# A decoder layer on one core: u also stored by columns, weights stored in the pieces read, three halves of the expert sums kept in PSUM

## The chip, the core and the metric

The kernel runs on one core of a Trainium2 chip. The metric is the device time of one execution in microseconds (us): three runs of the kernel before took 3350.16, 3357.07 and 3360.35 us, median 3357.07. The core has five engines that work side by side, each on its own list of instructions in a fixed order: TensorE (PE, matrix products), VectorE (DVE), ScalarE (ACT), GpSimd (POOL) and SyncE (SP, which here only issues transfers). Sixteen DMA engines move data between DRAM and the core's two memories, SBUF (128 partitions) and PSUM (eight banks of 128 x 512 float32, where PE writes its sums).

## The reference

One layer for 1024 tokens of 1024 values, in float32:

```python
h += W_out [ RMSNorm(attention) ; RMSNorm(convolution) ]      # both from RMSNorm(h) @ w_in
h += PEER(RMSNorm(h))
h += sigmoid(RMSNorm(h) @ w_ple_gate) * (p @ w_ple_proj)
out = RMSNorm(h)
```

PEER is a retrieval among 16384 single-neuron experts. Per token, each of 8 heads scores 2 x 128 keys (`xn @ peer_wq`, then a product with the keys), takes the 16 best of each half and then the 16 best of their sums; these 128 experts per token have gates g by a softmax. The result is

```python
h_e   = xn . u[e]                      # u: 16384 x 1024
y     = sum over the token's experts of gelu(h_e) * g_e * v[e]
```

The arrays are handed to the kernel by the host; what the host does to their layout before the launch is not part of the time.

## The kernel before

The 1024 tokens are 8 tiles of 128. Five groups of tiles (0; 1, 2; 3, 4; 5, 6; 7) go through the **front** one after the other: input projection (`qkv`, `convolve`), attention, convolution, output projection (`project`), key search (`search`) and the choice of experts (`combine`). Each product with a weight reads the weight afresh for the group, in pieces of 512 KB, three buffers (`w_piece`, L246). `token_major` (L254) reads 256 rows by 512 columns as [128, 2, 512], so runs of 512 columns, 2 KB, in DRAM; `channel_major` (L267) reads 1024 rows by 128 columns as [128, 8, 128], so runs of 512 B.

PEER is done in two ways. For tiles 0, 1, 2 and 7 (`FEW`) the experts are **gathered** (`gather_u` L602, `gather_v` L619): one indirect DMA from POOL's queue (L595) brings for each of the 128 tokens one row of u or v, 4 KB each, 512 KB in all, into one of six buffers, and DVE multiplies and sums it (L608 for u, L624 for v). That is 128 gathers of u and then 128 of v per tile, 1024 in all. Each use is put at least five gathers behind its own (`LAG`).

For tiles 3 to 6 (`ALL`) **all experts run** (`dense`, L695): 512 tokens against 128 chunks of 128 experts. Beforehand each tile's gates are laid into a matrix in DRAM (`gate_matrix`, L636). For float32 accuracy at a faster product, both sides of each product are split into a high and a low part, and three products are summed. A chunk needs

- `columns` (L702): the chunk's rows of u are loaded (512 KB), transposed by PE in eight blocks of 128 x 128 into two PSUM banks (`put`, L710), and each half is split by ACT (`uh`, L712) and DVE (`ul`, L714) into three buffers of half a chunk for each part. It is called one chunk ahead of its use;
- 24 products into a PSUM bank `ph` (L738 to L740), a gelu by ACT (L742), the gates by DVE (L746), a split of the result (`ah` L748, `al` L750);
- the chunk's rows of v, loaded into one of two buffers and split (`vh` L756, `vl` L758).

After every four chunks (a group of the dense sums, 32 in all) the sums over these 512 experts are made for 4 tiles x 2 halves of 512 columns, 12 products each (L769 to L771). Seven of these eight halves go through two PSUM banks `py` and are added to h by DVE each time (L773); one, tile 3's first half, stays in its own bank `kept_y` through all 32 groups and is added once (L774).

At the last group, `read` (L894) frees the inputs' memory and loads the last weights (`wt`). The **tail** is `embed` (L776) for each tile: a transposed and normed h (`pt_ple`, L792, evicted as `x3T`), 16 products per half with the gate's weight (`plg`, L802) and 4 with p (`plp`, L808) as the profile counts them, sigmoid, product, norm, output. For the dense tiles its PSUM tiles come from four banks that the inputs of the last sums leave; for the gathered tiles everything goes through the one bank `acc`. The gathered tiles 0 to 2 are embedded in the middle of the dense sums, with weights loaded for them (`we`).

The order on each engine and in each DMA queue is not written out by hand: a planner (the tile framework) makes it before the launch from the order of the program, priorities, buffers and estimated costs. The gathers are written last in the program, so they are fitted in where the rest leaves room; the engines then follow that order and wait where data or a buffer is not there.

Of the kernel before, what the change touches and what calls it, by code (L numbers as in the profile page):

```python
# [20 lines left out]
P = 128  # L21
# [4 lines left out]
GROUPS = ((0,), (1, 2), (3, 4), (5, 6), (7,))  # tiles of 128 tokens that go through the mixers together  # L26
# [4 lines left out]
FEW = (0, 1, 2, 7)  # tiles whose experts are gathered  # L31
ALL = (3, 4, 5, 6)  # tiles for which all experts run
# [19 lines left out]
GROUP = 4  # chunks of 128 experts whose outputs are summed in PSUM  # L52
BT = 32  # tokens of a block of the gate matrix
# [3 lines left out]
# Of the sums of two sorted lists of 16, the 16 largest lie where (i + 1) * (j + 1) <= 16.  # L57
# [14 lines left out]
def _constants():  # L72
    c = np.zeros((P, C_END), np.float32)
    # Columns of key blocks, the farthest first: distance of query q from key column s.
    dist = np.arange(P)[:, None] + (SEQ - P) - np.arange(SEQ)[None, :]
    mult = np.zeros(dist.shape)
    for window, step in PATTERNS:
        mult += (dist >= 0) & (dist <= window) & (dist % step == 0)
    c[:, C_BIAS : C_BIAS + SEQ] = np.where(mult > 0, math.sqrt(DH) * np.log(np.maximum(mult, 1)), NEG)
    c[:, C_ID : C_ID + P] = np.eye(P)  # L80
    c[:, C_IOTA : C_IOTA + P] = np.arange(P)
    freq = np.float32(THETA) ** (-np.arange(0, 2 * ROT, 2, dtype=np.float32) / np.float32(2 * ROT))
    c[:, C_FREQ : C_FREQ + ROT] = freq
# [19 lines left out]
def tile_layer(ctx, tc, t, consts, out):  # L103
# [7 lines left out]
    by_k = lambda name: t[name][0].rearrange("(k p) c -> p k c", p=P)  # L111
    w_in, w_out, w_q, w_g, w_p = (by_k(n) for n in ("w_in", "w_out", "peer_wq", "w_ple_gate", "w_ple_proj"))
# [28 lines left out]
    def rstd(srcs, n, name, junk=None, pool=small):  # L141
        """1 / sqrt(mean(src^2) + eps) along the free axis, a column for each src."""
# [13 lines left out]
    def transpose_to(dst, src, n, name, ps_tile, gain=None):  # L156
        """dst [P, n, P] = the n blocks of src [P, n * P], transposed; times gain [P, n]."""
# [35 lines left out]
    def load_tables():  # L193
        # Rows to columns: the gains of the mixers' norms, the convolution's taps and bias.
# [8 lines left out]
        # Rotary angles, brought into [-pi, pi] by exact multiples of parts of 2 pi.  # L203
# [42 lines left out]
    def w_piece(src, name):  # L246
        """A piece of a weight: [P, k, columns] in 4 KB of each partition."""
        _, k, c = src.shape
        w = mpool.tile([P, 1024], F32, tag="w", name=name, bufs=3)
        w = w.rearrange("p (k c) -> p k c", k=k)  # L250
# [53 lines left out]
    def qkv(g, xT):  # L304
# [16 lines left out]
        token_major(xT, w_in, DA, f"k{g}", done_k)  # L321
        token_major(xT, w_in, 0, f"q{g}", done_q)
        token_major(xT, w_in, 2 * DA, f"v{g}", lambda j, a: S.copy(vt[:, GROUPS[g][j], :], a))
        return qT

    def convolve(g, xT):
        """The gated units, channels on partitions, and the convolution's taps over them."""
        gn = xT.shape[2]
        glus = []
        for c in range(NCT):  # L330
            pg = channel_major(xT, w_in, 3 * DA + DC + c * P, f"gt{g}_{c}")
            sg = mpool.tile([P, GN], F32, tag="t2", name=f"sg{g}_{c}", bufs=3)[:, :gn]
            S.activation(sg, pg, AF.Sigmoid)
            pa = channel_major(xT, w_in, 3 * DA + c * P, f"a{g}_{c}")
# [28 lines left out]
    def attend(g, qT):  # L363
        """One softmax over the keys, each counted as often as the patterns hold it."""
# [42 lines left out]
    def mixed(g, ys, cT):  # L407
        """Both halves of the mixers' output, normed and transposed."""
# [31 lines left out]
    def project(g, yT):  # L440
        """h1 = x + y @ w_out."""
# [8 lines left out]
        for f in range(2):  # L450
            token_major(
                yT, w_out, f * 512, f"o{g}_{f}", lambda j, a: V.tensor_tensor(h1[j][:, half(f)], a, h1[j][:, half(f)], ALU.add)
# [15 lines left out]
    def search(g, x2T):  # L468
        """The 16 best keys of each head's halves."""
# [6 lines left out]
        for hp in range(PH // 2):  # L476
            qT = []
            for r in range(4):
                n = 4 * hp + r
                pq = channel_major(x2T, w_q, n * P, f"pq{g}_{n}")  # L480
# [19 lines left out]
    def combine(nm, vals, idxs, opool, gbufs):  # L500
        """For one tile: i1, i2 (bf16) and gates (f32), [P, head, rank]."""
# [24 lines left out]
        # Gates: softmax over the 16.  # L526
# [7 lines left out]
        # From a candidate's place to its row i and column j, then to the keys there.  # L534
# [8 lines left out]
        def total(dst, a, dt=BF16):  # L543
            """The sums over the last axis; its partial sums of more than two terms are of type dt."""
# [13 lines left out]
        # Row i: the number of starts up to the place; sums over the steps from one row to the next.  # L558
# [60 lines left out]
    def gather_v(i, ex, act, y):  # L619
        """The sum over experts of their rows of v, a rank of all tokens at a time."""  # L620
# [15 lines left out]
    def gate_matrix(gp, j, i1, i2, gate):  # L636
        """G[i1, i2, token] of one tile in DRAM, in blocks of BT tokens: each token's gates at its experts."""
# [42 lines left out]
    def wide_input(h1, xh, xl):  # L680
        """The normed input of the tiles for which all experts run, transposed, as a sum of two float32r."""
# [13 lines left out]
    def dense(du, dp, dus, dps, h1, xh, xl, read):  # L695
        """h1 += PEER(xn), over all experts, GROUP chunks of 128 at a time."""
        phs, puts, pys = bank(dus, "ph", 2), bank(dus, "put", 2), bank(dps, "py", 2)
        # One tile's sums stay in PSUM through all chunks; its halves come where the others' banks are emptied.
        kept_y = dps.tile([P, 512], F32, name="kept_y")
        order = [(1, 0), (1, 1), (0, 1), (2, 0), (0, 0), (2, 1), (3, 0), (3, 1)]  # L700

        def columns(c):  # L702
            """The chunk's rows of u, transposed, as a sum of two float32r: halves of the k blocks."""
            u = du.tile([P, D], F32, tag="u", name=f"u{c}", bufs=2)
            nc.sync.dma_start(u, u_d[rows(c), :])
            uh, ul = [], []
            for b in range(0, KD, 4):
                pt = puts(f"put{c}_{b}")
                for i in range(4):
                    nc.tensor.transpose(pt[:, rows(i)], u[:, rows(b + i)], ident)  # L710
                hi = du.tile([P, 512], F32R, tag="uh", name=f"uh{c}_{b}", bufs=3)
                S.copy(hi, pt)  # L712
                lo = du.tile([P, 512], F32R, tag="ul", name=f"ul{c}_{b}", bufs=3)
                V.tensor_tensor(lo, pt, hi.bitcast(F32), ALU.subtract)  # L714
                uh.append(hi)
                ul.append(lo)
            return uh, ul

        ready = columns(0)
        for c0 in range(0, NK, GROUP):  # L720
# [10 lines left out]
            for c in range(c0, c0 + GROUP):  # L731
# [4 lines left out]
                for k in range(KD):  # L736
                    hi, lo = uh[k // 4][:, rows(k % 4)], ul[k // 4][:, rows(k % 4)]
# [25 lines left out]
            for j, f in order:  # L763
                py = kept_y if (j, f) == (0, 0) else pys(f"py{c0}_{j}_{f}")
                for e in range(GROUP):
                    first, last_e = e == 0, e == GROUP - 1
                    if (j, f) == (0, 0):
# [4 lines left out]
                if (j, f) != (0, 0):  # L772
                    V.tensor_tensor(h1[j][:, half(f)], py, h1[j][:, half(f)], ALU.add)  # L773
        V.tensor_tensor(h1[0][:, half(0)], kept_y, h1[0][:, half(0)], ALU.add)  # L774

    def embed(pool, bufs, i, h, g_fin, ps_tile, weight):  # L776
        """out = finalnorm(h + sigmoid(rmsnorm(h) @ w_g) * (p @ w_p)) for one tile; weight(k, f): rows 2k of both, a half."""
# [6 lines left out]
        # Transposed and divided by the root mean square by a product with a diagonal matrix.  # L784
# [11 lines left out]
        for f in range(2):  # L796
            pg = ps_tile(f"plg{i}_{f}")
# [7 lines left out]
            pp = ps_tile(f"plp{i}_{f}")  # L805
# [10 lines left out]
    def embed_weight(pool, name, kq, f, bufs=1):  # L816
        w = pool.tile([P, 2, 512], F32, tag=name.rstrip("0123456789") if bufs > 1 else name, name=f"{name}_{kq}_{f}", bufs=bufs)
        nc.sync.dma_start(w, w_p[:, :, half(f)] if kq == KD // 2 else w_g[:, 2 * kq : 2 * kq + 2, half(f)])
        return w

# [73 lines left out]
    def read():  # L894
        """What follows takes the place of the inputs of the last sums, beside which it starts."""
# [8 lines left out]
        tails.extend((tail, bank(tail_ps, "pg", 4)))  # L904
# [4 lines left out]
    tiles = [embed(tails[0], ND, ALL[j], h1[j], g_fin, tails[1], lambda k, f: kept[k, f]) for j in range(ND)]  # L909
    # As they are done: the front of a tile's work beside the sums of the next, then the products.  # L910
    for j in (1, 0, 2, 1, 0, 3, 2, 3):
        next(tiles[j])
    for i, y in gather_all():
        with tc.high_priority():
# [4 lines left out]
            for _ in embed(ep, 1, i, y, g_fin, acc, weight):  # L919
                pass  # L920
# [3 lines left out]
    "x", "p", "positions", "norm_mix", "w_in", "conv_w", "conv_b", "conv_ln_g", "conv_ln_b", "g_attn_out", "g_conv_out",  # L924
    "w_out", "norm_ffn", "peer_wq", "sub_keys", "expert_u", "expert_v", "norm_ple", "w_ple_gate", "w_ple_proj", "final_norm",
]

# [19 lines left out]
```

## Time and profile before

| | |
|---|---|
| median of three runs | 3357.07 us (3350.16 to 3360.35) |
| span of the profiled execution, first to last instruction | 3356.7 us (the page gives no other time of it) |
| PE busy | 2938.0 us, 88% |
| DVE busy | 2675.1 us, 80% |
| POOL busy | 1615.9 us, 48% |
| ACT busy | 1222.0 us, 36% |
| moved by DMA | 901.62 MB, 268 GB/s over the span |

A row of the costliest groups gives line, engine, operation, `out<-in`, shapes and count, then the busy time in us and the mean in ns, then the idle time of the engine right before these instructions and what ended most of it. PE's durations there overlap, since matmuls are pipelined; starts in the timeline tell the pace. A row of waits reads: who waited <- for whom: us in total, times, longest. A row of stretches gives start and end, length, then busy us (and instructions) of the engines that the text names, TensorE's granted clock (1 is full), the mean busy share of the DMA engines and GB/s. A row of the chain of waits gives start, length and the work that the end hung on at that time. The 40 slices are of 84 us, each digit the busy share in tenths.

### The profile page before, as it was taken

The numbers are of one execution on the slowest core, as the hardware profiler recorded it, in microseconds if no ns is written. First come the engines' busy times: TensorE is split into PE (matmuls) and PEld (weight loads), VectorE is DVE, ScalarE is ACT, GpSimd is POOL, SyncE is SP. The second block draws the span as 40 slices with busy tenths as digits, with TensorE's granted clock in tenths as the row PEclk, the third lists the DMA queues.
The fourth block names the chain that finished last, engine by engine and source line by source line (L and its number), as shares of the span: only waits on it lengthen the run. The fifth ranks groups of instructions, "written<-read, shape, count | busy, mean of one in ns | idle before, by whom it ended". The sixth has DMA issues, their size and how long they took to land.

```text
span 3356.7 us, 39363 instructions
## 1 busy us (share of the span) xinstructions
PE 2938.0 (88%) x12867; PEld 2253.1 (67%) x12867; DVE 2675.1 (80%) x5416; ACT 1222.0 (36%) x2316; POOL 1615.9 (48%) x1392
## 2 busy tenths in 40 slices
PE   6687888799789399978999999798999989999998
PEld 3454366367457299966777777577877757777763
DVE  3269779989979766677899888688988978888882
ACT  4436335434534477742223223222222233222234
POOL 1237645443543543325565655454655645555650
PEclk9898989899899699979999999999999999999999
DMA  6575894594486364369999989998989999999880
GB/s 199 169 263 186 315 320 126 186 324 138 138 301 219 119 213 163 144 232 346 342 345 347 343 312 327 325 323 325 347 317 337 325 327 340 342 322 326 309 332 32
DMA packets 425439, 901.62 MB, mean 269 GB/s; under 512 B 27866, under 2 KB 217714, under 8 KB 423186
## 3 DMA queue, kind: packets, MB, share of 16 engines
q0 software_dynamic: 147456, 536.94, 44.2%
q1 hardware_dynamic: 274512, 358.81, 32.0%
q10 hardware_dynamic: 3266, 3.36, 0.3%
q8 instruction: 102, 1.67, 0.2%
q14 instruction: 103, 0.84, 0.1%
HBM read 857.06 MB, written 41.94 MB: 268 GB/s over the span
## 4 chain that ended last, share of the span: by engine, by line
PE 36%; DMA 20%; DVE 18%; issue 14%; POOL 9%; ACT 3%; POOLq 0%; ACTq 0%; SPq 0%; DVEq 0%
PE pG L676 7%; DMA v<-in_expert_v_dram 5%; PE pq L272 4%; DMA w_pq<-in_peer_wq_dram 3%; POOL v L595 3%; DVE cc L358 3%; POOL u L595 3%; DVE u L608 3%; DMA v<-in_expert_v_dram,ex 3%; PE plg L802 2%; DVE gy L624 2%; DMA u<-in_expert_u_dram,ex 2%; PE o L263 2%; PE py L769 2%; PE py L771 2%
## 5 line engine op out<-in xcount | busy, mean ns | idle before, releaser
L595 POOL DMA_INDIRECT u<-in_expert_u_dram,ex x512 | 640.5, 1251 | 710.3 <-DVE hk L608 458.5
L595 POOL DMA_INDIRECT v<-in_expert_v_dram,ex x512 | 661.5, 1292 | 593.5 <-DVE gy L624 433.5
L624 DVE SCALAR_TENSOR_TENSOR gy<-v,ga,gy 128x1024 f32<-128x1024 f32 x512 | 662.7, 1294 | 36.6 <-DMA v<-in_expert_v_dram,ex 29.0
L608 DVE CUSTOM_DVE_ANT_0 u<-u,gxn 128x1024 f32<-128x1024 f32 x512 | 619.1, 1229 | 35.2 <-DMA u<-in_expert_u_dram,ex 34.7
L738 PE MATMUL ph<-xh,uh 128*128 128x512 f32 x1024 | 427.3, 417 | 0.0
L739 PE MATMUL ph<-xl,uh 128*128 128x512 f32 x1024 | 415.2, 405 | 0.0
L740 PE MATMUL ph<-xh,ul 128*128 128x512 f32 x1024 | 414.4, 405 | 0.1
L756 ACT CAST vh<-v 128x1024 fp32r<-128x1024 f32 x128 | 131.5, 1052 | 701.5 <-PE py L771 522.1
L769 PE MATMUL py<-vh,ah 128*128 128x512 f32 x896 | 353.8, 396 | 9.8 <-ACT ah L748 8.3
L770 PE MATMUL py<-vl,ah 128*128 128x512 f32 x896 | 349.6, 393 | 0.0
L771 PE MATMUL py<-vh,al 128*128 128x512 f32 x896 | 348.1, 392 | 0.0
L352 POOL TENSOR_TENSOR side<-side,tap 128x256 f32<-128x256 f32 (+1 forms) x300 | 217.1, 725 | 184.5 <-ACT tap L351 166.3
L272 PE MATMUL pq<-x2T,w_pq 128*128 128x256 f32 (+1 forms) x1280 | 254.7, 350 | 35.4 <-DMA w_pq<-in_peer_wq_dram 35.3
L272 PEld LDWEIGHTS pq<-x2T,w_pq 128*128 128x128 f32 x1280 | 220.6, 200 | 60.7 <-DMA w_pq<-in_peer_wq_dram 16.6
L740 PEld LDWEIGHTS ph<-xh,ul 128*128 128x128 f32 x1024 | 200.4, 196 | 47.2 <-issue 2.7
L738 PEld LDWEIGHTS ph<-xh,uh 128*128 128x128 f32 x1024 | 202.4, 198 | 41.1 <-issue 2.2
L739 PEld LDWEIGHTS ph<-xl,uh 128*128 128x128 f32 x1024 | 201.2, 196 | 41.4 <-issue 2.7
L710 PE MATMUL put<-cst,u 128*128 128x128 f32 x1024 | 149.0, 285 | 89.4 <-DVE ul L714 77.0
L758 DVE TENSOR_TENSOR vl<-v,vh 128x1024 fp32r<-128x1024 f32 x128 | 156.0, 1219 | 75.0 <-ACT vh L756 74.4
L712 ACT CAST uh<-put 128x512 fp32r<-128x512 f32 x256 | 149.6, 584 | 167.9 <-PE ph L739 137.2
L769 PEld LDWEIGHTS py<-vh,ah 128*128 128x128 f32 x896 | 169.1, 189 | 55.5 <-ACT ah L748 16.1
L710 PEld LDWEIGHTS put<-cst,u 128*128 128x128 f32 x1024 | 124.3, 146 | 117.2 <-DVE ul L714 88.9
(264 smaller groups left out, 5223.1 us busy)
## 6 DMA issues: line engine op xcount, KB each, us to landing
u<-in_expert_u_dram SPq DMA_DIRECT2D x128, 512.0 KB
v<-in_expert_v_dram SPq DMA_DIRECT2D x128, 512.0 KB
w_pq<-in_peer_wq_dram SPq DMA_DIRECT2D x80, 512.0 KB
gate_d<-stage SPq DMA_DIRECT2D x16, 2048.0 KB
gt<-gate_d SPq DMA_DIRECT2D x64, 512.0 KB
w_o<-in_w_out_dram SPq DMA_DIRECT2D x40, 512.0 KB
we<-in_w_ple_gate_dram SPq DMA_DIRECT2D x24, 512.0 KB
w_k<-in_w_in_dram SPq DMA_DIRECT2D x20, 512.0 KB
```

The costliest lines, as they stand in the source:

```text
L272: nc.tensor.matmul(a, w[:, k, :], xT[:, k, :], start=k == 0, stop=k == KD - 1)
L595: d = G.indirect_dma_start(out=e, out_offset=None, in_=table, in_offset=bass.IndirectOffsetOnAxis(ap=index, axis=0))
L608: uses(V.tensor_tensor_reduce(out=e, in0=e, in1=xn, scale=1.0, scalar=0.0, op0=ALU.mult, op1=ALU.add, accum_out=hk[:, k : k + 1]))
L624: uses(V.scalar_tensor_tensor(y, e, act[:, k : k + 1], y, ALU.mult, ALU.add))
L676: nc.tensor.matmul(pg[:, rows(e)], o2[:, :, e], parts[e], start=True, stop=True)
L710: nc.tensor.transpose(pt[:, rows(i)], u[:, rows(b + i)], ident)
L738: nc.tensor.matmul(ph, hi, xh[:, k, :], start=k == 0, stop=False)
L739: nc.tensor.matmul(ph, hi, xl[:, k, :], start=False, stop=False)
L740: nc.tensor.matmul(ph, lo, xh[:, k, :], start=False, stop=k == KD - 1)
L769: nc.tensor.matmul(py, ah[e][:, rows(j)], vh[e][:, half(f)], start=first, stop=False)
L770: nc.tensor.matmul(py, ah[e][:, rows(j)], vl[e][:, half(f)], start=False, stop=False)
L771: nc.tensor.matmul(py, al[e][:, rows(j)], vh[e][:, half(f)], start=False, stop=last_e)
```

## The change

1. **u by columns.** Beside the rows of u (which the gathers still read) the host lays u out a second time, chunk by chunk, transposed: 128 partitions x 1024 values, one run of 4 KB for each partition. `columns` loads such a chunk and has no transposes; ACT and DVE split it as one piece of 128 x 1024 from SBUF, into two buffers of a whole chunk for each part. The two PSUM banks `put` are gone.
2. **Weights in pieces.** The host lays out every weight in the pieces that the kernel reads, each piece 128 partitions x 4 KB in one run. The pieces hold the same values, and as many are loaded as before.
3. **Three kept halves.** Tile 3's both halves and tile 6's first half stay in PSUM through all groups; five halves are added in each group and three once at the end. The order of the eight halves alternates kept and other ones in its middle.
4. **Banks of the tail.** The dense tiles' transposes get two banks instead of four; their products (and tile 7's) get four banks `late`, which come free when the banks of the dense sums are closed.

Comments are taken out as well, which changes no instruction. The diff, cut to its core:

```diff
+    uT_d = t["uT"]
-    by_k = lambda name: t[name][0].rearrange("(k p) c -> p k c", p=P)
-    w_in, w_out, w_q, w_g, w_p = (by_k(n) for n in ("w_in", "w_out", "peer_wq", "w_ple_gate", "w_ple_proj"))
+    w_qkv, w_ag, w_out, w_q, w_g, w_p = (t[n] for n in ("w_qkv", "w_ag", "w_out", "peer_wq", "w_ple_gate", "w_ple_proj"))
...
     def token_major(xT, w_k, c0, name, done):
-            w = w_piece(w_k[:, 2 * kq : 2 * kq + 2, c0 : c0 + 512], f"w_{name}_{kq}")
+            w = w_piece(w_k[c0, kq], f"w_{name}_{kq}").rearrange("p (i c) -> p i c", i=2)
...
     def channel_major(xT, w_k, c0, name):
-        w = w_piece(w_k[:, :, c0 : c0 + P], f"w_{name}")
+        w = w_piece(w_k[c0], f"w_{name}").rearrange("p (k c) -> p k c", k=KD)
...
     def dense(du, dp, dus, dps, h1, xh, xl, read):
-        phs, puts, pys = bank(dus, "ph", 2), bank(dus, "put", 2), bank(dps, "py", 2)
-        kept_y = dps.tile([P, 512], F32, name="kept_y")
-        order = [(1, 0), (1, 1), (0, 1), (2, 0), (0, 0), (2, 1), (3, 0), (3, 1)]
+        phs, pys = bank(dus, "ph", 2), bank(dps, "py", 2)
+        kept_y = {jf: dps.tile([P, 512], F32, name=f"kept_y{jf[0]}{jf[1]}") for jf in ((0, 0), (0, 1), (3, 0))}
+        order = [(1, 0), (1, 1), (0, 0), (2, 0), (0, 1), (2, 1), (3, 0), (3, 1)]
         def columns(c):
             u = du.tile([P, D], F32, tag="u", name=f"u{c}", bufs=2)
-            nc.sync.dma_start(u, u_d[rows(c), :])
-            uh, ul = [], []
-            for b in range(0, KD, 4):
-                pt = puts(f"put{c}_{b}")
-                for i in range(4):
-                    nc.tensor.transpose(pt[:, rows(i)], u[:, rows(b + i)], ident)
-                hi = du.tile([P, 512], F32R, tag="uh", name=f"uh{c}_{b}", bufs=3)
-                S.copy(hi, pt)
-                lo = du.tile([P, 512], F32R, tag="ul", name=f"ul{c}_{b}", bufs=3)
-                V.tensor_tensor(lo, pt, hi.bitcast(F32), ALU.subtract)
-                uh.append(hi)
-                ul.append(lo)
-            return uh, ul
+            nc.sync.dma_start(u, uT_d[c])
+            hi = du.tile([P, D], F32R, tag="uh", name=f"uh{c}", bufs=2)
+            S.copy(hi, u)
+            lo = du.tile([P, D], F32R, tag="ul", name=f"ul{c}", bufs=2)
+            V.tensor_tensor(lo, u, hi.bitcast(F32), ALU.subtract)
+            return hi, lo
...
-                if (j, f) != (0, 0):
+                if (j, f) not in kept_y:
                     V.tensor_tensor(h1[j][:, half(f)], py, h1[j][:, half(f)], ALU.add)
-        V.tensor_tensor(h1[0][:, half(0)], kept_y, h1[0][:, half(0)], ALU.add)
+        for (j, f), py in kept_y.items():
+            V.tensor_tensor(h1[j][:, half(f)], py, h1[j][:, half(f)], ALU.add)
-    def embed(pool, bufs, i, h, g_fin, ps_tile, weight):
+    def embed(pool, bufs, i, h, g_fin, ps_tile, ps_out, weight):
-            pg = ps_tile(f"plg{i}_{f}")
+            pg = ps_out(f"plg{i}_{f}")
-            pp = ps_tile(f"plp{i}_{f}")
+            pp = ps_out(f"plp{i}_{f}")
...
-        tails.extend((tail, bank(tail_ps, "pg", 4)))
+        tails.extend((tail, bank(tail_ps, "pg", 2)))
     dense(du, dp, dus, dps, h1, xh, xl, read)
     den_ps.close()
     den.close()
-    tiles = [embed(tails[0], ND, ALL[j], h1[j], g_fin, tails[1], lambda k, f: kept[k, f]) for j in range(ND)]
+    late_ps = ctx.enter_context(tc.tile_pool(name="late_ps", bufs=1, space=PSUM))
+    late = bank(late_ps, "late", 4)
+    tiles = [embed(tails[0], ND, ALL[j], h1[j], g_fin, tails[1], late, lambda k, f: kept[k, f]) for j in range(ND)]
...
-            for _ in embed(ep, 1, i, y, g_fin, acc, weight):
+            for _ in embed(ep, 1, i, y, g_fin, acc, late if i == FEW[-1] else acc, weight):
...
+def _by_token(w):
+    k, c = w.shape
+    return w.reshape(k // 256, 2, P, c // 512, 512).transpose(3, 0, 2, 1, 4).reshape(c // 512, k // 256, P, 1024)
+def _by_channel(w):
+    k, c = w.shape
+    return w.reshape(k // P, P, c // P, P).transpose(2, 1, 0, 3).reshape(c // P, P, k)
...
+    give("w_qkv", _by_token(w_in[:, : 3 * DA]))
+    give("w_ag", _by_channel(w_in[:, 3 * DA :]))
+    for name in ("w_out", "w_ple_gate", "w_ple_proj"):
+        give(name, _by_token(np.asarray(inputs[name])[0]))
+    give("peer_wq", _by_channel(np.asarray(inputs["peer_wq"])[0]))
+    give("uT", _by_channel(np.asarray(inputs["expert_u"])[0].T))
```

More of the change, by code (lines that the diff above doesn't have):

```diff
@@ L246, in w_piece @@
     def w_piece(src, name):
-        _, k, c = src.shape
         w = mpool.tile([P, 1024], F32, tag="w", name=name, bufs=3)
-        w = w.rearrange("p (k c) -> p k c", k=k)
         nc.sync.dma_start(w, src)
@@ L319, in done_q @@
             transpose_to(qT[:, j], q, H // 2, f"q{i}", tps)
-        token_major(xT, w_in, DA, f"k{g}", done_k)
-        token_major(xT, w_in, 0, f"q{g}", done_q)
-        token_major(xT, w_in, 2 * DA, f"v{g}", lambda j, a: S.copy(vt[:, GROUPS[g][j], :], a))
+        token_major(xT, w_qkv, 1, f"k{g}", done_k)
+        token_major(xT, w_qkv, 0, f"q{g}", done_q)
+        token_major(xT, w_qkv, 2, f"v{g}", lambda j, a: S.copy(vt[:, GROUPS[g][j], :], a))
         return qT
@@ L330, in convolve @@
         for c in range(NCT):
-            pg = channel_major(xT, w_in, 3 * DA + DC + c * P, f"gt{g}_{c}")
+            pg = channel_major(xT, w_ag, NCT + c, f"gt{g}_{c}")
             sg = mpool.tile([P, GN], F32, tag="t2", name=f"sg{g}_{c}", bufs=3)[:, :gn]
             S.activation(sg, pg, AF.Sigmoid)
-            pa = channel_major(xT, w_in, 3 * DA + c * P, f"a{g}_{c}")
+            pa = channel_major(xT, w_ag, c, f"a{g}_{c}")
             glu = apool.tile([P, TAPS - 1 + GN], F32, tag="glu", name=f"glu{g}_{c}", bufs=NCT - 1)[:, : TAPS - 1 + gn]
@@ L451, in project @@
             token_major(
-                yT, w_out, f * 512, f"o{g}_{f}", lambda j, a: V.tensor_tensor(h1[j][:, half(f)], a, h1[j][:, half(f)], ALU.add)
+                yT, w_out, f, f"o{g}_{f}", lambda j, a: V.tensor_tensor(h1[j][:, half(f)], a, h1[j][:, half(f)], ALU.add)
             )
@@ L479, in search @@
                 n = 4 * hp + r
-                pq = channel_major(x2T, w_q, n * P, f"pq{g}_{n}")
+                pq = channel_major(x2T, w_q, n, f"pq{g}_{n}")
                 q = mpool.tile([P, GN], F32, tag="pqT", name=f"pqT{g}_{n}", bufs=4)[:, :gn]
@@ L736, in dense @@
                 for k in range(KD):
-                    hi, lo = uh[k // 4][:, rows(k % 4)], ul[k // 4][:, rows(k % 4)]
+                    hi, lo = uh[:, rows(k)], ul[:, rows(k)]
                     nc.tensor.matmul(ph, hi, xh[:, k, :], start=k == 0, stop=False)
@@ L763, in dense @@
             for j, f in order:
-                py = kept_y if (j, f) == (0, 0) else pys(f"py{c0}_{j}_{f}")
+                py = kept_y[j, f] if (j, f) in kept_y else pys(f"py{c0}_{j}_{f}")
                 for e in range(GROUP):
                     first, last_e = e == 0, e == GROUP - 1
-                    if (j, f) == (0, 0):
+                    if (j, f) in kept_y:
                         first, last_e = first and c0 == 0, last_e and c0 + GROUP == NK
@@ L817, in embed_weight @@
         w = pool.tile([P, 2, 512], F32, tag=name.rstrip("0123456789") if bufs > 1 else name, name=f"{name}_{kq}_{f}", bufs=bufs)
-        nc.sync.dma_start(w, w_p[:, :, half(f)] if kq == KD // 2 else w_g[:, 2 * kq : 2 * kq + 2, half(f)])
+        nc.sync.dma_start(w.rearrange("p i c -> p (i c)"), w_p[f, 0] if kq == KD // 2 else w_g[f, kq])
         return w
@@ L918, in tile_layer @@
                 weight = lambda k, f: kept[k, f]
-            for _ in embed(ep, 1, i, y, g_fin, acc, weight):
+            for _ in embed(ep, 1, i, y, g_fin, acc, late if i == FEW[-1] else acc, weight):
                 pass
 _INS = [
-    "x", "p", "positions", "norm_mix", "w_in", "conv_w", "conv_b", "conv_ln_g", "conv_ln_b", "g_attn_out", "g_conv_out",
-    "w_out", "norm_ffn", "peer_wq", "sub_keys", "expert_u", "expert_v", "norm_ple", "w_ple_gate", "w_ple_proj", "final_norm",
-]
+    "x", "p", "positions", "norm_mix", "conv_w", "conv_b", "conv_ln_g", "conv_ln_b", "g_attn_out", "g_conv_out",
+    "norm_ffn", "sub_keys", "expert_u", "expert_v", "norm_ple", "final_norm",
+]
+def _by_token(w):
[4 more added lines that the diff above has]
+    return w.reshape(k // P, P, c // P, P).transpose(2, 1, 0, 3).reshape(c // P, P, k)
 def kernel(**inputs):
@@ L934, with give @@
     arrays, t = {}, {}
-    for name in _INS:
-        a = np.ascontiguousarray(inputs[name])
+    def give(name, a):
+        a = np.ascontiguousarray(a)
         arrays[f"in_{name}_dram"] = a
         t[name] = nc.dram_tensor(f"in_{name}_dram", a.shape, mybir.dt.from_np(a.dtype), kind="ExternalInput").ap()
+    for name in _INS:
+        give(name, inputs[name])
+    w_in = np.asarray(inputs["w_in"])[0]
+    give("w_qkv", _by_token(w_in[:, : 3 * DA]))
[4 more added lines that the diff above has]
+    give("uT", _by_channel(np.asarray(inputs["expert_u"])[0].T))
     c = _constants()
```

## The prediction

> **What bounds the kernel now.** I read the slices of the page first, since the kernel has two halves: up to slice 17 the mixers, the search and the gate matrix, from 1460 us on the sums over all experts (dense) with the gathers beside them.
>
> ```profile
> span 3356.7 us, 39363 instructions
> PE   6687888799789399978999999798999989999998
> DVE  3269779989979766677899888688988978888882
> DMA  6575894594486364369999989998989999999880
> GB/s 199 169 263 186 315 320 126 186 324 138 138 301 219 119 213 163 144 232 346 342 345 347 343 312 327 325 323 325 347 317 337 325 327 340 342 322 326 309 332 32
> ```
>
> From slice 18 on PE, DVE and DMA are all near full, so no one of them can be shortened alone. I took 1460 to 3241 (the last of the dense sums) and what follows in one view of stretches, then the same for the gather's line, then PE's waits of the first stretch.
>
> ```profile
> 1460.00:3241.00 1781.00, 1641.28 (x7343) 1319.59 (x7344) 1535.91 (x2194) 471.98 (x735) 977.63 (x753) 0.96 0.92 329
> 3241.00:3357.00 116.00, 98.66 (x290) 48.80 (x289) 46.99 (x55) 44.20 (x90) 14.28 (x14) 0.96 0.33 130
> ```
> ```profile
> 1460.00:3241.00 1781.00, 977.63 (x753) 0.96 0.92 329
> 1180.00:1460.00 280.00, 17.60 (x14) 0.97 0.46 171
> ```
> ```profile
> PE put L710 <- DVE ul L714: 77.0, 36, 5.4
> ```
>
> The columns are PE, PEld, DVE, ACT, POOL, clock, DMA share and GB/s. DVE is busy 1535.9 of 1781 us, 86%. Of the gathers 753 are issued in this stretch and 14 after it; 257 came before. The matmuls themselves are plain in the timeline of one group of four chunks:
>
> ```profile
> 2321.66 1.03 PE L710 MATMUL put<-cst,u 128*128 128x128 f32 x8
> 2322.45 0.48 PE L738 MATMUL ph<-xh,uh 128*128 128x512 f32 x1
> ...
> 2328.01 1.03 PE L710 MATMUL put<-cst,u 128*128 128x128 f32 x8
> ...
> 2340.38 1.11 PE L710 MATMUL put<-cst,u 128*128 128x128 f32 x4 [5.44 <-DVE ul L714]
> ```
>
> Eight transposes take 2321.66 to 2322.45, 0.79 us, and the 24 matmuls of a chunk 2322.45 to 2328.01, 5.56 us, 0.232 each; the page's mean of 417 ns counts overlap. So the 6144 large matmuls hold PE about 6144 x 0.232 = 1425 us, the transposes 128 x 0.79 = 101, the wait for the split 77. After the dense sums PE still has the last products:
>
> ```profile
> 3277.97 1.04 ACT sqj_ple L146 x2
> 3283.21 2.07 PE pt_ple L792 x8
> 3288.36 9.44 PE plg L802 x22
> 3338.40 6.87 PE plg L802 x16
> 3345.27 1.73 PE plp L808 x4
> 3347.09 0.70 DVE sg L809
> ```
> ```profile
> 3267.77 1.86 POOL L595 DMA_INDIRECT v<-in_expert_v_dram,ex  x1 [0.65 <-DVE gy L624]
> ```
> ```profile
> 3275.09 1.28 DVE L624 SCALAR_TENSOR_TENSOR gy<-v,ga,gy 128x1024 f32<-128x1024 f32 x1
> ```
>
> The last gather is used up at 3276.4, and the kernel ends 80 us later: not because of that tile but because five tiles' products (two halves of 6.87 + 1.73 us each) stand in line on PE behind the dense sums, 115.7 us from 3241 to the end. So today the end is set by PE, with the gathers close behind. The span lies 0.4 us under the median of the runs, 3357.07; the sum below is made on the span and the 0.4 is dropped.
>
> **The change part by part.** **PE** loses the 1024 transposes, 101 us. The wait of `put` for `ul` has no transposes left to stall; what remains of it is a wait of `ph` for `ul`, one chunk later in PE's order. Nothing of it may go, or all 77 us; the late event is the split, which comes no sooner, but 5.56 us of matmuls now stand before the place where PE needs it, and the longest wait was 5.4. I take two thirds, 50 us. Dense sums then end at 3241 - 101 - 50 = 3090 (bounds 3063 and 3140).
>
> **Splitting u** moves from PSUM halves to whole rows in SBUF. The durations of that are the ones v has already, same shape and place:
>
> ```profile
> L714 DVE TENSOR_TENSOR ul<-put,uh 128x512 fp32r<-128x512 f32 x256 | 175.0, 684 | 21.1 <-ACT uh L712 20.6
> L758 DVE TENSOR_TENSOR vl<-v,vh 128x1024 fp32r<-128x1024 f32 x128 | 156.0, 1219 | 75.0 <-ACT vh L756 74.4
> L712 ACT CAST uh<-put 128x512 fp32r<-128x512 f32 x256 | 149.6, 584 | 167.9 <-PE ph L739 137.2 <-PE put L710 24.1 <-issue 4.3
> L756 ACT CAST vh<-v 128x1024 fp32r<-128x1024 f32 x128 | 131.5, 1052 | 701.5 <-PE py L771 522.1 <-DMA v<-in_expert_v_dram 179.4
> L773 DVE TENSOR_TENSOR h<-py,h 128x512 f32<-128x512 f32 x224 | 153.0, 686 | 30.1 <-PE py L771 29.4 <-issue 0.3
> ```
>
> DVE: 256 x 0.684 becomes 128 x 1.219, 19 us less. ACT: 256 x 0.584 becomes 128 x 1.052, 15 us less on an engine at 472 of 1781, worth nothing in time. The chain from a landed u to a usable pair grows from 1.27 us (a half) to 2.27; hidden behind the 5.56 us of the chunk before, since two whole buffers replace three halves (ACT's 137 us of waiting for `ph` is that third half being held). Without the cover it costs 128 x 1.0 = 128 us. In ACT's queue the casts of v, which wait for DMA, may stand ahead of it, as today; who waits then is `ul`, then PE. SP issues the same 128 loads of u, but the buffer is now given back by `ul`, not by the transposes, so SP's later loads of v and gates stand behind that; with two buffers it is a chunk ahead.
>
> **Kept sums**: seven additions of 0.686 us in each of 32 groups become five, and three at the end for one: 225 become 163, 42.5 us less DVE. With 19 that is 61.5 us.
>
> **The gathers** fill what DVE has left. At the same 86.2% DVE does 1630 x 0.862 = 1405 us of work up to 3090, and 1535.9 - 61.5 = 1474 are due: 69 us short. One gather costs DVE about 1.3 us:
>
> ```profile
> L595 POOL DMA_INDIRECT v<-in_expert_v_dram,ex x512 | 661.5, 1292 | 593.5 <-DVE gy L624 433.5
> L624 DVE SCALAR_TENSOR_TENSOR gy<-v,ga,gy 128x1024 f32<-128x1024 f32 x512 | 662.7, 1294 | 36.6 <-DMA v<-in_expert_v_dram,ex 29.0
> ```
> ```profile
> POOL v L595 <- issue: 61.9, 203, 0.3
> ```
> ```profile
> 130.00:140.00 10.00, 7.19 (x54) 6.90 (x52) 0.00 (x0) 2.06 (x6) 0.00 (x0) 0.84 0.97 313
> 210.00:220.00 10.00, 10.00 (x28) 4.30 (x26) 7.95 (x18) 1.32 (x3) 7.39 (x6) 1.00 1.03 406
> 3250.00:3260.00 10.00, 10.00 (x25) 4.41 (x24) 6.42 (x5) 1.78 (x2) 4.70 (x5) 1.00 1.04 401
> ```
>
> So 53 more are left over, 67 with the 14. Alone they run at between 1.29 us (DVE) and 2.0 (five in 3250 to 3260, beside weights); POOL's 1.29 and 0.3 between two make 1.6, which I take, as it holds in either case. Last issue 3090 + 107 = 3197, landing and use 8 more (3268 to 3276 today), 3205. Then tile 7's products alone: 5.2 us to its first `pt_ple`, 5.2 to its products, 2 x 8.6, and 9.6 from 3347.09 to the end, 37 us: 3242. The others' products end before: 3090 + 115.7 = 3206. How early the dense sums end hardly matters to this sum: each us taken from them leaves 0.66 gathers more, at 1.6 us each. Up to 3126 the gathers come last.
>
> **The tail's banks**: two for transposes instead of four, and products that wait until the sums' banks are emptied, the three kept ones among them (3 x 0.686). A delay of 0 to 8 us on PE, 3 taken, covered by the 36 us between 3206 and 3242; at full price if the products come last again. Behind the waiting products on PE stand the fronts of the later tiles and of tile 7.
>
> **Weights in pieces**: by the code 24 pieces of each of five groups (w_pq, w_a, w_gt) are read in runs of 512 B and the rest in runs of 2 KB; all become 4 KB. PE waits for them, mostly before 1460 us:
>
> ```profile
> PE pq L272 <- DMA w_pq<-in_peer_wq_dram: 35.3, 13, 11.9
> PE o L263 <- DMA w_o<-in_w_out_dram: 19.2, 12, 5.2
> ```
> ```profile
> 161.93 5.39 DMA w_pq<-in_peer_wq_dram
> ...
> 478.43 10.92 DMA w_pq<-in_peer_wq_dram
> ```
>
> The short runs (w_pq, 130 to 140) go at 313 / 0.97 = 323 GB/s per full share, long ones (3250 to 3260) at 401 / 1.04 = 386, and the 2 KB runs among gathers (210 to 220) no slower than that. So only the 512 B ones gain, 16% of a landing of 5.39 to 10.92 us, up to 1.7 us at 13 waits: 20 us, of which I keep 15, as DVE and its order share that half's length. Bounds: nothing, and the 54.5 us of the two rows; a loss if the order shifts, as much again as 15.
>
> The Trainium skill, "DMA: Bandwidth & Descriptors" (Specifications), says that transfers from 512 B up run at line rate; by that no piece gains and the sum is 15 us higher. The stretch at 313 GB/s with a share of 0.97 speaks against it, so I keep the 15.
>
> **Sum**: 3242 - 15 = 3227 us.
>
> **Rivals.** *The order stays.* If each group keeps as many gathers as now, DVE paces the dense sums and everything moves by its saving alone, 61.5 / 0.862 = 71 us: 3357 - 71 - 15 = 3271. For it: DVE at 86% in every stretch. Against: gathers are emitted last and only fill gaps, and PE's shorter group leaves fewer.
>
> *The gathers keep up.* Then PE's products come last: 3206 - 15 = 3191. It needs 329 x 1.781 + 130 x 0.116 = 601 MB in some 1640 us, 366 GB/s; no slice is over 347, though 401 occurs without dense loads.
>
> *Gathers left behind* (slower). The order is planned, not found at run time: in 1180 to 1460 it let through only 14 of them, with DVE at six tenths in those slices. If it fills DVE less in the shorter groups, the rest runs alone at 1.6 us. From a share of 80% (1304 us done, 131 + 14 left, 232 us) nothing is gained; at 76% 195 are left, 312 us, and the end is 3090 + 312 + 45 - 15 = 3432.
>
> *Nothing comes of it*: the same at about 80%, 3350.
>
> **How the numbers follow.** Forecast 52%, order stays 22%, gathers keep up 15%, left behind 6%, nothing 5%. A run of this kernel tells 0.3%, 10 us, from no change. Faster is the first three and two of the last five, 91%; same 3%; slower 6%. The range goes from 3165, the keeping up with 26 us more from the weights, to 3315, the order kept with nothing from the weights and 30 us of delay from split or banks.
>
> **What would show it.** Right: no wait of PE on `ul` above some 30 us in all; dense sums ending 120 to 180 us earlier; a stretch of gathers without dense sums; the last use of a gather about 40 us before the end; `pq` waiting some 20 us for its pieces. Wrong: `ph` waiting for `ul` in every chunk, over 100 gathers behind the dense sums, or products last on PE again.

## The result, and the profile after

The changed kernel takes 3254.68 us (median of four runs, 3251.5 to 3265.54) against 3358.71; the ratio is 0.9699, 95% interval 0.9671 to 0.9727. The forecast was 3227 us, range 3165 to 3315: the time lies in the range, 28 us above the forecast. The profiled execution is the longest of the four, 3265.54 us, with a span of 3263.7; the steps below are read from it.

The page's head, then the stretches that answer to those of before (PE, PEld, DVE, ACT, POOL, clock, DMA share, GB/s), then the same for the gathers' line alone:

```profile
span 3263.7 us, 37043 instructions
PE   6697898899797599978999999899999997999952
DVE  3379789889989766686888888778988886889895
```
```profile
1421.00:3063.00 1642.00, 1519.64 (x6319) 1196.41 (x6320) 1386.51 (x1903) 449.81 (x599) 905.46 (x669) 0.97 0.93 330
...
3150.00:3229.00 79.00, 0.00 (x0) 0.00 (x0) 69.79 (x56) 2.00 (x5) 56.05 (x49) 0.50 0.93 343
```
```profile
1421.00:3063.00 1642.00, 905.46 (x669) 0.97 0.93 330
3063.00:3264.00 201.00, 114.96 (x98) 0.75 0.79 289
```

The half before the dense sums is 39 us shorter (1460 to 1421), the dense sums themselves 139 us (1781 to 1642). (Counted from their first product, as in the table of the experiments, it is 41 and 137.) But 98 gathers stand behind them instead of 14. The timeline of PE shows what that does to the end; the chain of waits and the timelines of POOL and DVE give the last gathers (landing, last issue, last uses):

```profile
3063.11 0.39 PE L762 MATMUL py<-vh,al 128*128 128x512 f32 x1
...
3144.73 1.88 PE L800 MATMUL plp<-wt,pTt 128*128 128x512 f32 x4
3231.15 2.08 PE L784 MATMUL pt_ple<-dg,gy 128*128 128x128 f32 x8 [84.53 <-ACT dg L779]
```
```profile
3217.71 7.22 DMA v<-in_expert_v_dram,ex
```
```profile
3220.35 1.02 POOL L593 DMA_INDIRECT v<-in_expert_v_dram,ex  x1 [0.30 <-issue]
```
```profile
3225.03 3.93 DVE L622 SCALAR_TENSOR_TENSOR gy<-v,ga,gy 128x1024 f32<-128x1024 f32 x3 [0.77 <-DMA v<-in_expert_v_dram,ex]
```

The four dense tiles' products are done at 3146.6; then PE has nothing for 84.53 us, until the last gather is used up at 3229.0 and tile 7 can be finished, 34.7 us before the end. Before, the end hung on PE's products; now it hangs on the gathers, as forecast. PE's waits in the dense stretch, after and before (the wait of `put` before is in the prediction):

```profile
PE py L760 <- ACT ah L739: 51.9, 30, 4.1
PE ph L731 <- DVE ul L707: 24.5, 22, 2.1
```
```profile
PE py L769 <- ACT ah L748: 8.3, 13, 1.0
```

And the pieces that replaced the halves of u:

```profile
L707 DVE TENSOR_TENSOR ul<-u,uh 128x1024 fp32r<-128x1024 f32 x128 | 155.9, 1218 | 10.9 <-ACT uh L705 10.7
L705 ACT CAST uh<-u 128x1024 fp32r<-128x1024 f32 x128 | 134.4, 1050 | 135.2 <-PE ph L730 93.3 <-DMA u<-in_uT_dram 41.0
L764 DVE TENSOR_TENSOR h<-py,h 128x512 f32<-128x512 f32 x160 | 107.8, 686 | 61.0 <-PE py L762 55.9 <-issue 4.4
```

### The profile page after: what moved, and what is told of

Read it like the earlier page. It is cut to its first block, busy times and chain, and to the rows that moved or that the text cites. A ratio compares the mean times of both kernels' runs of the same rounds, so it can differ in the third digit from the quotient of the medians.

```text
span 3263.7 us, 37043 instructions
## 1 busy us (share of the span) xinstructions
PE 2814.0 (86%) x11843; PEld 2126.9 (65%) x11843; DVE 2633.1 (81%) x5226; ACT 1198.8 (37%) x2180; POOL 1650.2 (51%) x1392
## 4 chain that ended last, share of the span: by engine, by line
PE 33%; DVE 25%; DMA 16%; issue 15%; POOL 8%; ACT 3%; ACTq 0%; POOLq 0%; SPq 0%; DVEq 0%
PE pG L674 7%; DMA v<-in_expert_v_dram 5%; POOL v L593 4%; DVE cc L356 4%; DVE gy L622 3%; DMA v<-in_expert_v_dram,ex 3%; DVE u L606 3%; PE py L760 2%; PE py L762 2%; PE py L761 2%; PE pq L270 2%; DVE ul L707 2%; POOL u L593 2%; PE o L261 2%; PE kept_y L760 2%
## 5 line engine op out<-in xcount | busy, mean ns | idle before, releaser
L593 POOL DMA_INDIRECT u<-in_expert_u_dram,ex x512 | 672.9, 1314 | 679.3 <-DVE hk L606 428.2
L731 PE MATMUL ph<-xh,ul 128*128 128x512 f32 x1024 | 407.6, 398 | 24.9 <-DVE ul L707 24.5
L729 PE MATMUL ph<-xh,uh 128*128 128x512 f32 x1024 | 404.1, 395 | 14.8 <-ACT uh L705 14.8
L730 PE MATMUL ph<-xl,uh 128*128 128x512 f32 x1024 | 403.8, 394 | 0.0
L760 PE MATMUL py<-vh,ah 128*128 128x512 f32 x640 | 257.4, 403 | 51.9 <-ACT ah L739 51.9
L761 PE MATMUL py<-vl,ah 128*128 128x512 f32 x640 | 255.1, 401 | 0.0
L762 PE MATMUL py<-vh,al 128*128 128x512 f32 x640 | 253.7, 403 | 0.0
L705 ACT CAST uh<-u 128x1024 fp32r<-128x1024 f32 x128 | 134.4, 1050 | 135.2 <-PE ph L730 93.3
L760 PEld LDWEIGHTS py<-vh,ah 128*128 128x128 f32 x640 | 122.0, 191 | 90.7 <-ACT ah L739 64.6
L663 POOL TENSOR_TENSOR ob<-o,gT 128x512 f32<-128x512 bf16 x64 | 96.6, 1509 | 165.2 <-PE pG L674 142.1
L739 ACT CAST ah<-gelu 128x512 fp32r<-128x512 f32 x128 | 79.2, 620 | 273.3 <-DVE gelu L737 270.4
```

The source lines that it names most:

```text
L593: d = G.indirect_dma_start(out=e, out_offset=None, in_=table, in_offset=bass.IndirectOffsetOnAxis(ap=index, axis=0))
L729: nc.tensor.matmul(ph, hi, xh[:, k, :], start=k == 0, stop=False)
L730: nc.tensor.matmul(ph, hi, xl[:, k, :], start=False, stop=False)
L731: nc.tensor.matmul(ph, lo, xh[:, k, :], start=False, stop=k == KD - 1)
L760: nc.tensor.matmul(py, ah[e][:, rows(j)], vh[e][:, half(f)], start=first, stop=False)
L761: nc.tensor.matmul(py, ah[e][:, rows(j)], vl[e][:, half(f)], start=False, stop=False)
```

## The experiments

Three questions: what each part is worth alone; whether the gathers really set the end now and PE's products before; and what decides how many gathers stay behind. Times are medians, ratios are to the kernel before on the same chip (the first row is of the chip of E9 to E12; on the others its median was 3358.4 to 3358.9). "First half" is the time up to the first product of the dense sums, "left" the gathers issued after their last product, both from the profiled run.

| run | us | ratio, 95% | first half | dense sums | left | last product to end |
|---|---|---|---|---|---|---|
| before | 3357.8 | 1 | 1468 | 1773 | 14 | 116 |
| changed | 3254.7 | 0.9699 (0.9671 to 0.9727) | 1428 | 1636 | 98 | 201 |
| E1 weights | 3327.5 | 0.9911 (0.9876 to 0.9945) | 1431 | 1759 | 15 | 115 |
| E2 only the 512 B runs | 3322.7 | 0.9888 (0.9833 to 0.9943) | 1443 | 1769 | 14 | 118 |
| E3 u by columns | 3291.5 | 0.9797 (0.9769 to 0.9826) | 1463 | 1611 | 103 | 216 |
| E4 changed, one kept half | 3264.6 | 0.9711 (0.9684 to 0.9738) | 1444 | 1628 | 103 | 205 |
| E5 E4, transposes again | 3308.8 | 0.9851 (0.9801 to 0.9902) | 1429 | 1758 | 22 | 113 |
| E6 changed, 64 gathers out | 3169.3 | 0.9431 (0.9394 to 0.9468) | 1431 | 1616 | 35 | 114 |
| E7 lead 4 | 3256.3 | 0.9678 (0.9631 to 0.9724) | 1472 | 1671 | 30 | 119 |
| E8 lead 3 | 3292.0 | 0.9787 (0.9745 to 0.983) | 1490 | 1688 | 6 | 117 |
| E9 lead 5, then 4 | 3233.5 | 0.9632 (0.9588 to 0.9676) | 1443 | 1650 | 54 | 135 |
| E10 four kept halves | 3231.8 | 0.9632 (0.9591 to 0.9673) | 1437 | 1626 | 75 | 164 |
| E11 E9 and E10 | 3214.2 | 0.9571 (0.9532 to 0.961) | 1431 | 1666 | 33 | 117 |
| E12 before, 64 gathers out | 3354.3 | 0.9981 (0.9956 to 1.0006) | 1471 | 1790 | 0 | 95 |

### E1 and E2: the weights alone

Before's `w_piece` reads host-made pieces; in E2 only the channel-major ones (w_pq, w_a, w_gt).

```diff
-            w = w_piece(w_k[:, 2 * kq : 2 * kq + 2, c0 : c0 + 512], f"w_{name}_{kq}")   # E1 only
+            w = w_piece(w_k[c0, kq], f"w_{name}_{kq}")
-        w = w_piece(w_k[:, :, c0 : c0 + P], f"w_{name}")                                # E1 and E2
+        w = w_piece(w_k[c0], f"w_{name}", KD)
```

> Only the weights are laid out in the pieces read; u, the transposes, the kept half and the tail's banks are as before. Theory: the half before the dense sums is 39 us shorter, as in the changed kernel (1460 to 1421), and all that follows moves with it, because the same 257 gathers are done by then: about 3318 us, and PE waits for w_pq under 8 us instead of 35. Rival: the shorter first half only hands its gathers on to the second, or came from the planner's new order and not from the pieces: within 15 us of before.

> Only w_pq, w_a and w_gt (runs of 512 B before) are laid out in pieces; the weights read in runs of 2 KB stay. Theory: the 512 B runs carry the loss, since PE's waits fell from 35.3 to 4.7 us there and only from 19.2 to 14.8 on w_o: at least 28 of the 39 us, about 3328 us. Rival, by the rule that runs from 512 B up go at line rate: nothing, 3357 us, and the gain of the first run lies in the 2 KB pieces.

E1 gained 31 us, E2 36; their intervals overlap, so the 2 KB runs were worth nothing that can be told beside the 512 B runs. On every engine and queue the instructions of both stand in the same order as before's, so this is not the planner. PE's waits of the first half in E2, and landings on the chain of E2, the first three without gathers beside them and the others with:

```profile
PE o L263 <- DMA w_o<-in_w_out_dram: 21.0, 13, 5.0
PE pq L272 <- DMA w_pq<-in_w_pqp_dram: 5.6, 7, 2.1
```
```profile
137.69 5.12 DMA w_pq<-in_w_pqp_dram
144.93 5.88 DMA w_pq<-in_w_pqp_dram
162.05 3.99 DMA w_pq<-in_w_pqp_dram
...
469.56 8.80 DMA w_pq<-in_w_pqp_dram
...
990.04 7.14 DMA w_pq<-in_w_pqp_dram
```

The first three landings took 7.15, 6.40 and 5.39 us before: a fifth less. But PE's wait for w_pq fell from 35.3 to 5.6 us, and the chain that had twelve such landings from 132 us on has five. The likely reason is the three buffers, by which a landing that is a little shorter than the work on the pieces ahead of it isn't waited for at all; no run here varies them.

### E3, E4 and E5: u, the kept halves and PE's transposes

E3 is before with `columns` as in the change. E4 is the changed kernel with `kept_y` for (0, 0) alone and the order of the halves as before. E5 adds to E4 the transposes, into two banks `put` that nobody reads:

```diff
-        kept_y = {...  for jf in ((0, 0), (0, 1), (3, 0))}
+        kept_y = {...  for jf in ((0, 0),)}                                             # E4, E5
-        order = [(1, 0), (1, 1), (0, 0), (2, 0), (0, 1), (2, 1), (3, 0), (3, 1)]
+        order = [(1, 0), (1, 1), (0, 1), (2, 0), (0, 0), (2, 1), (3, 0), (3, 1)]        # E4, E5
...
             nc.sync.dma_start(u, uT_d[c])
+            for b in range(0, KD, 4):                                                   # E5
+                pt = puts(f"put{c}_{b}")
+                for i in range(4):
+                    nc.tensor.transpose(pt[:, rows(i)], u[:, rows(b + i)], ident)
```

> Only u by columns: no transposes, u split as a whole from SBUF; weights, one kept half and four tail banks as before. Theory (the gathers end last, so only DVE's work counts): PE's 101 us of transposes go, the dense sums end 100 to 140 us earlier, but DVE is only 19 us freer, so over 100 gathers are left over at 1.58 us each: 3335 to 3357 us. Rival (PE's work sets the end): 101 us of transposes and most of the 77 us of stall show in the time, 3220 to 3260 us.

> The changed kernel with one kept half instead of three (order of the halves as before). 62 additions of 0.686 us more on DVE, PE's work the same. Theory: 42.5 us of DVE work push 33 gathers behind the dense sums, 1.58 us each: 52 us more than the changed kernel, about 3306 us. Rival: the additions sit in DVE's gaps while it waits for the casts of v: within 10 us of the changed kernel, 3245 to 3265 us.

> The changed kernel with one kept half, and u's 128 x 8 transposes done again by PE into two PSUM banks that nobody reads: PE's work is back, DVE's and ACT's are those of the run with one kept half (3264.6 us). The planned order now holds 22 to 23 gathers in a group instead of 20. Prediction's theory (an earlier end of the dense sums is given back by gathers left over): dense sums 100 us longer, but only some 40 gathers left behind them instead of 103, end within 20 us of 3265. Rival (PE's work shows in the time in full): 3365 us. Between them, if gathers run at one per 2.45 us in the dense sums and per 1.58 us alone: 100 us more of dense sums less 41 gathers at 1.58, 3300 us.

E3 met neither: 67 us of gain, between the two. Its dense sums are 162 us shorter, its gathers left 103, not many more than the changed kernel's 98, though its DVE has 42.5 us more to do. E4 says the same more plainly. The stretch of its dense sums, and the changed kernel's:

```profile
1443.50:3071.80 1628.30, 1513.03 (x6320) 1194.02 (x6321) 1412.56 (x1954) 451.11 (x601) 913.61 (x665) 0.98 0.93 331
```
```profile
1427.60:3063.10 1635.50, 1519.74 (x6319) 1196.49 (x6320) 1380.01 (x1895) 448.86 (x599) 905.18 (x669) 0.97 0.93 331
```

62 additions more, and DVE simply is busier, 1412.6 instead of 1380.0 us in a stretch no longer; 665 gathers fit in instead of 669. The two times differ by 10 us and their intervals overlap: of the 52 us expected nothing certain is there. So the gathers do not fill what DVE has left. In DVE's instruction list most groups of the dense sums hold 20 gathers (18 to 21) in both kernels, and 22 to 23 in before and in E5, where PE has the transposes. E1's 31 us and E3's 67 add up to 98 of the 104 of the whole change, so little is left for the other two parts.

E5 lengthens the dense sums by 129 us and takes 81 gathers off those left. The start of the last use of a gather hardly moves, 3240.9 to 3233.9 (E5's dense sums also start 14 us earlier), but the end of the profiled run is 3187.2 plus 113 us of PE's products; by the medians E5 takes 44 us more than E4. The figure between the theories, 3300, was nearest.

```profile
1429.40:3187.20 1757.80, 1620.85 (x7338) 1299.85 (x7337) 1508.39 (x2036) 445.64 (x598) 1018.15 (x746) 0.98 0.93 331
3187.20:3300.20 113.00, 98.11 (x290) 48.23 (x288) 55.12 (x60) 38.89 (x86) 24.27 (x22) 0.96 0.43 159
```
```profile
PE put L707 <- DMA u<-in_uT_dram: 25.2, 20, 2.5
```

Not all of the 129 us are PE's work: PE is busy 108 us more (1620.85 against 1513.03) and idle 22 us more, since here it is the transposes that wait for u to land.

### E6 and E12: what ends last

```diff
-        for k in range(SLOTS):
+        for k in range(SLOTS // 2 if i == FEW[-1] else SLOTS):
             e = fetch(v_d, ex[:, k : k + 1], f"v{i}_{k}")
```

> The changed kernel without the last 64 gathers of v of tile 7 (its sum over experts is incomplete, so is that tile's output); all else in the same order. Theory (the gathers end last): the last use of a gather comes 64 x 1.58 = 101 us earlier, at some 3128, and then PE's products, which end at 3146, come last with tile 7's behind them: 3160 to 3180 us. Rival (PE or something else sets the end): 3245 to 3255 us.

> The kernel before without the last 64 gathers of v of tile 7 (that tile's output is incomplete). Theory (before, PE's products end last, 115 us behind the dense sums, and the gathers 80 us before the end): the last use of a gather comes about 100 us earlier and the time falls by little, 0 to 25 us for the last groups' freer DVE: 3333 to 3358 us. Rival (the gathers set the end there too): 3258 us.

The same 64 gathers are worth 85 us in the changed kernel (3254.7 to 3169.3) and 3.5 us in before, within its interval. In E12 the last gather is used at 3143.2 instead of 3276.4, 133 us sooner, and the end stays; tile 7's products now run ahead of the last dense sums (7393 instructions of PE in that stretch instead of 7336), which is why only 95 us follow them. Before, PE's products set the end; in the changed kernel the gathers do, until in E6 the products take over: 114 us behind the dense sums, as before. The stretches behind the dense sums, E6 and E12:

```profile
3046.30:3160.50 114.20, 99.41 (x290) 49.20 (x288) 71.51 (x75) 40.47 (x90) 40.56 (x35) 0.94 0.59 221
```
```profile
3260.90:3355.90 95.00, 79.11 (x234) 40.11 (x232) 17.60 (x26) 32.44 (x68) 0.00 (x0) 0.93 0.06 22
```

### E7 to E11: fewer gathers left

If the planned order leaves gathers behind, another order should bring them in. `LAG` is the lead, in gathers, by which a row is planned ahead of its use.

```diff
-LAG = 5
+LAG = 4                                                    # E7; 3 in E8
...
-        for ins in users.pop(len(fetches) - 1 - LAG, ()):
+        lag = LAG if len(fetches) <= 2 * SLOTS else LAG - 1        # E9, E11
+        for ins in users.pop(len(fetches) - 1 - lag, ()):
...
-        phs, pys = bank(dus, "ph", 2), bank(dps, "py", 2)
-        kept_y = {...  for jf in ((0, 0), (0, 1), (3, 0))}
-        order = [(1, 0), (1, 1), (0, 0), (2, 0), (0, 1), (2, 1), (3, 0), (3, 1)]
+        phs, pys = bank(dus, "ph", 2), bank(dps, "py", 1)          # E10, E11
+        kept_y = {...  for jf in ((0, 0), (0, 1), (3, 0), (3, 1))}
+        order = [(1, 0), (0, 0), (1, 1), (0, 1), (2, 0), (3, 0), (2, 1), (3, 1)]
```

> The changed kernel with the use of a row planned four gathers behind its own instead of five. The planned order then has 276 uses ahead of the dense sums instead of 254, 21 to 22 in a group instead of 20, and 43 behind them instead of 112. Theory (the planned order, not DVE's room, leaves gathers behind, and they are what ends last): 69 gathers fewer at 1.58 us, less some 30 us of longer dense sums: about 3180 to 3210 us. Rival (DVE has no more room, or the rows land too late for the shorter lead): dense sums longer by as much as is saved, DVE waiting for rows over 60 us, 3250 us or more.

> As before with a lead of three gathers: 288 uses ahead of the dense sums, 19 behind them. Theory: little more than with four, since PE's products then come last: 3180 to 3215 us. Rival: rows land 7 to 12 us after issue, three leads are some 5 us, DVE waits in each use and the dense sums grow by more than 100 us: 3280 us or more.

E7 left 30 gathers instead of 98, as the theory had it, and gained nothing: its first half is 44 us longer with 22 gathers more in it, its dense sums 35 us, and 119 us behind these PE's products end last. E8 the same, further: 62 and 53 us longer. Both times are those of the rivals. DVE's waits for rows between 1430 and 3060 us are 56.5 us in E7, against 26.5 in the changed kernel: 30 us more, so the rival's late rows are a part of the 79 us, not the whole:

```profile
DVE u L606 <- DMA u<-in_expert_u_dram,ex: 38.7, 58, 2.7
...
DVE gy L622 <- DMA v<-in_expert_v_dram,ex: 17.8, 38, 1.6
```

> The changed kernel with the lead of five gathers kept for tile 0, whose gathers fill the half before the dense sums, and four for the tiles gathered beside the dense sums. Planned order: 254 uses ahead as in the changed kernel, 21 to 22 in a group, 67 behind instead of 112. Theory (with four everywhere the gain was eaten by the first half, 44 us longer with 22 gathers more in it): first half 1430 us as in the changed kernel, dense sums some 30 us longer, 45 gathers fewer behind them, end about 3220 us, with gathers and PE's products ending close together. Rival (the dense sums grow by as much as the gathers left behind shrink, or PE's products last): 3245 us or more.

> The changed kernel with four halves kept (also tile 6's second) and one bank for the four others, kept and other ones by turns. 32 additions less on DVE (22 us); planned order with 21 gathers in a group instead of 20 and 89 behind instead of 112. Theory: 23 gathers fewer behind, some 15 us of longer dense sums: about 3230 us. Rival: with one bank PE waits after each half that is not kept until DVE has added it, 0.69 us and what stands ahead of it, say 1 us more than the 2.7 us of the kept half between: 128 us, 3330 us or more.

> Both of these: four kept halves and the lead of four beside the dense sums. Planned order with 22 to 23 gathers in a group, 46 behind. Theory: the gathers end before PE's products, so the end is dense sums plus 117 us; some 3205 to 3225 us, no more than 15 us better than either alone. Rival: as for the two.

E9 has a first half of 1443 us, against 1472 in E7, and takes in 713 gathers beside the dense sums, 44 more than the changed kernel, for 14 us more of them; 54 are left, and the time is 13 us above the theory's. E10 takes in 693 in 1626 us; PE's waits on the one bank come to 6.1 us in all, not 128:

```profile
PE py L760 <- DVE h L764: 6.1, 7, 2.5
```

E11 is the best version, 3214.2 us, 0.9571 of before against 0.9699 of the changed kernel; the intervals do not touch, while those of E9 and of E10 alone still touch the changed kernel's. E11's gathers end at 3162, 51 us before the end; PE's products end last again, so both are near balance. The dense sums of E9, then those of E11 and what follows them:

```profile
1442.80:3092.70 1649.90, 1514.47 (x6319) 1190.22 (x6320) 1435.99 (x1938) 445.46 (x595) 955.91 (x713) 0.98 0.95 342
```
```profile
1430.50:3096.60 1666.10, 1529.70 (x6319) 1200.12 (x6320) 1443.69 (x1930) 443.20 (x593) 991.17 (x735) 0.97 0.96 345
3096.60:3213.20 116.60, 99.11 (x290) 48.67 (x288) 69.27 (x74) 43.02 (x91) 38.72 (x33) 0.95 0.55 208
```

## Why the prediction was right, and where it was not

| step | predicted | in the changed kernel |
|---|---|---|
| first half | 15 us less | 39 less |
| dense sums | 1630 | 1642 |
| gathers left, at | 67, 1.6 us | 98, 157 / 98 = 1.60 us |
| last issue to last use | 8 | 9 |
| tile 7's products to the end | 37 | 35 |
| span | 3227 | 1421 + 1642 + 157 + 9 + 35 = 3264 |

**PE and the transposes.** Right that PE's work falls by the transposes, and too small: of the 139 us, 122 are busy time of PE (1641.28 to 1519.64, with modelled ends of the products) where the sum had 101; with the transposes back (E5) it is 108. Why PE's work fell by more than that stays open. Of the two thirds of the 77 us of stall the mechanism held but the gain did not: `ul` is waited for 24.5 us, about the third that I left, but PE now waits 51.9 us for `ah` instead of 8.3. 77.0 and 8.3 before, 24.5 and 51.9 now: most of the wait moved, and PE's idle time in the stretch fell by 17 us (139.7 to 122.4), not by 50. In ACT's list `ah` waits for DVE's product with the gates (270.4 us in all, 195.9 before), which stands among gathers; that the faster `ph` merely uncovered this is argued, not shown. That the sum still came within 12 us is in part luck: one term too small, one too large.

**Splitting u.** Right: 1.05 and 1.218 us, as v's rows had it; the chain is hidden but for the 24.5 us of waits for `ul`.

**Kept sums.** The count was right, 163 additions at 0.686 us. Their worth of 42.5 us of DVE, carried into the gathers, was not: E4 has five gathers more behind the dense sums, not 33, and differs by 10 us that can't be told from nothing. A fourth half, for which the planned order took a gather more into each group, did count (E10, 23 us with it; E10 also has another order of the halves and one bank less for the others).

**The gathers.** The step that failed is that the gathers "fill what DVE has left", at "the same 86.2%": DVE did 1386.5 of 1642, 84.4%, and 98 were left instead of 67, 50 us of the sum. E4 shows the reason: how many go into a group is set in the planned order, 20 in it whether DVE has 62 additions more or not, and E9 shows that DVE, with the same additions, had room for 44 more (713 against 669) in dense sums 14 us longer. How the planner comes to its number was not tested. "The order stays" did not come about (20 in a group, 22 to 23 before); of "gathers left behind" the mechanism came in a mild form, 98 of the 145 or so that would have cost the whole gain.

**What ends last.** Right on both sides: PE's products before (E12), the gathers after (E6), with the 37 us of the tail. The 1.6 us for a gather came out as a mean of unlike parts, which is luck: six were issued in the first 15 us, 2.5 each, and 45 in the last 65 us, when nothing else runs beside them, 1.44 each. There POOL takes 1.13 us for an issue and pauses 0.30 us before each, so the reason given for the price holds and its size, from 1.29, does not:

```profile
3063.00:3078.00 15.00, 5.96 (x6) 0.77 1.03 409
...
3157.00:3222.00 65.00, 50.97 (x45) 0.50 0.98 361
```

The claim that an earlier end of the dense sums hardly matters as long as it lies before some 3126 us holds too: 129 us of dense sums moved the last gather by 7 us (E5; 81 gathers, 0.63 for each us where the sum had 0.66), and E5 lost time because its dense sums end at 3187 and the products come last.

**Weights.** Right in place, too small by half: 31 and 36 us alone, 39 in the profile, instead of 15. The term took 16% off each landing at 13 waits and then kept three quarters; the waits for w_pq did not shrink by a share but went away (35.3 to 5.6 us). That DVE's order would hold back a part was wrong. The Trainium skill ("DMA: Bandwidth & Descriptors", Specifications) gives 512 B as the least transfer for line rate. By that rule longer runs would have gained nothing; E2 measured 36 us (1.1%, 0.6 to 1.7) for 512 B runs made 4 KB, so for these pieces the measurement decides against it.

**Banks of the tail.** Not seen in the time: the tail behind the last gather is 34.7 us; no run undid this part alone.

## What to carry to other kernels

When two streams of work share engines, ask which of them ends last after the change, not only before: between E5 and E4 129 us came off the dense sums and a third of it showed, because the gathers' end hardly moved. Where a planner fixes the order, free time on an engine is not filled by itself; count in the instruction list how much of the second stream it lets in, and tune that together with the change (E11, with a fourth kept half: 40 us). A small cut in a landing can remove most of a wait, as for w_pq here.

## What was not expected of the hardware

That 512 B runs cost so much more than their share of the transfer rate: a fifth of the landing, but 30 us of waits, 26 of the 35.3 us being in 300 to 600 and 900 to 1180, where gathers run beside them (600 to 900, with gathers too, has 3.8). And that gathers alone, with six buffers, go at one in 1.44 us, 361 GB/s and a DMA share of 0.98, while DVE needs 1.3: there POOL never waits for a buffer, only its own 1.13 us and the 0.30 between.
